# Context steps pinned behind the expert tile they are written beside, with other weights for the steps

## The chip, the cores and the metric

The kernel runs on one core of one Trainium2 chip. The metric is the time of one execution on the device in microseconds (us); the median of a few runs counts. PE or TensorE is the matrix engine, PEld its weight load, DVE, ACT and POOL are the vector, scalar and GpSimd engines, and SP is the queue that issues the loads of the weights.

## What is computed

Two blocks run one behind the other on 256 tokens of width 1024, in float32. The first mixes the tokens (mLSTM and Hyena) and ends in a mixture of 16 experts; each expert takes 32 tokens:

```python
aff = jax.nn.softmax((xn @ w_router).astype(jnp.float32), axis=-1)
g, idx = lax.top_k(jnp.swapaxes(aff, 1, 2), cap)
xs = xn[bidx, idx]
hid = jax.nn.silu(jnp.einsum('becd,edf->becf', xs, w_gate)) * jnp.einsum('becd,edf->becf', xs, w_up)
y = jnp.einsum('becf,efd->becd', hid, w_down) * g[..., None].astype(xn.dtype)
```

The second block has two layers and takes a context of 256 tokens beside the tokens `x`. Layer 0 carries the context through the whole layer, layer 1 only needs its keys and values:

```python
mod_c = silu_cc @ w_ada[l] + b_ada[l]
o, oc = token_mixers(modulate(x, sh1, sc1), modulate(xc, sh1c, sc1c), ...)
if ctx_out:
    xc = layer_norm(DEEPNORM_ALPHA * xc + g1c * (oc @ w_out[l]), ln1_g[l], ln1_b[l])
    xc = layer_norm(DEEPNORM_ALPHA * xc + g2c * swiglu(modulate(xc, sh2c, sc2c), ...), ln2_g[l], ln2_b[l])
```

`token_mixers` holds two softmax attentions of three pairs of heads each and a gated linear attention between them. The context depends on nothing that the first block computes.

## The kernel before, in words

The program has three stages. `phase_a` is the mixing of the first block, up to the router's scores. Then the experts and the context run together, driven by `run` (L446 to L486). Then `x_path` (L1906) is the second block for the tokens.

The expert stage. `moe` (L1112) is a generator: for each expert, 8 tiles of `w_gate`, 8 of `w_up` and 8 of `w_down`, 384 tiles in all, each 128 x 2048 floats (1 MB). A tile is loaded by `etile` into one of seven buffers (`w`, four, and `wb`, three) and used by four products of 32 x 512 (`xsel` or `hidT` against the tile), which appear in the profile as eight; after each tile `moe` yields. Between two experts `combine` (L1166) adds the result to the tokens (`Yh` and `Yl` against `PT`).

The context. `ctx_path` (L1874) is a generator too. First it runs what `self.later` still holds: the modulation vectors of both blocks (`modvec`, L399), for which tiles of `w_ada` (0.5 MB) go through four buffers `wm`. Then come the context's projections, the linear attention (`gla`, L1680, eight levels, each with keys scaled on DVE, POOL and ACT before TensorE makes the scores), the pairs of softmax attention (`pair_attn`, L1391: scores, softmax on DVE and ACT, `turn` for the transposes, `av` for the values), the output projection, a layer norm (`lnT`, L1183: `colsum`, `rows`, `colsum`, `rows`), the feed-forward part and another layer norm. Each part yields a number before it writes its instructions: what it is worth in expert tiles, where 1.43 make one tile.

`run` interleaves both in the text: after each expert tile it takes steps of the context until their sum has reached the share that belongs to the tile. That is only the order of writing. A scheduler behind it then orders the instructions of each engine by what it expects to be ready, so a step of the context may move ahead of expert tiles beside or before which it was written. Each engine executes its own list in order; SP issues the loads in its order, and one load that waits for a free buffer holds up those behind it. `issue_after(x)` makes the instructions that a block writes on the engine of `x` stand behind `x` in that list; other engines are not touched.

The names in the profile: `w` and `wb` are expert tiles, `wm` tiles of the context and of the modulation, `lhs` the modulation's input, `xsel` the chosen tokens, `hid` and `hidT` an expert's hidden values, `E` the scaled keys of the linear attention, `Pm` the softmax, `nak`, `naq`, `nav` and `gak`, `graw`, `gav` keys, queries and values of both attentions, `inv` the constant of the norm's sums, `nm` and `lnr` its means and roots.

Of the kernel before, what the change touches and what calls it, by code (L numbers as in the profile page):

```python
# [218 lines left out]
class _B:  # L219
# [104 lines left out]
    def T(self, pool, shape, tag, bufs=1, dt=F32):  # L324
        self.n += 1
        return pool.tile(shape, dt, tag=tag, name=f"{tag}_{self.n}", bufs=bufs)

    def P(self, tag):
        self.n += 1
        return self.pp.tile([128, 512], F32, tag=tag, name=f"ps{self.n}", bufs=self.pbufs[tag])  # L330
# [115 lines left out]
    def run(self):  # L446
        nc, tc, d = self.nc, self.tc, self.d
        self.wbufs = {"w": 4, "wm": 4, "wx": 2, "wb": 3, "wd": 2, "split": 4}
        with ExitStack() as es:
            E = lambda **k: es.enter_context(tc.tile_pool(**k))  # L450
            self.cp = E(name="cp", bufs=1)
            self.res = E(name="res", bufs=1)
            pm, pa = "b", "a"
            self.ws = E(name="ws", bufs=5, side="right")
            with tc.tile_pool(name="ps", bufs=1, space=PSUM) as self.pp, \
                    tc.tile_pool(name="wm", bufs=4, side="right") as self.wm:
                self.pbufs = {"b": 2, "a": 3, "g": 2, "f": 1}
                self.setup()
                with tc.tile_pool(name="A", bufs=1) as ap:
                    self.wx = ap  # L460
                    self.phase_a(ap, pm, pa)
                    self.wx = None
                if self.stop == "A":
                    return
                kp = E(name="kv", bufs=1)
                self.kvpool(kp)
                with tc.tile_pool(name="M", bufs=1) as mp, tc.tile_pool(name="WB", bufs=1) as self.wb:
                    self.moe_route(mp, pm)
                    with tc.tile_pool(name="X", bufs=1, side="right") as xp:

                        g = self.ctx_path(xp, pa)
                        done, total = 0.0, 480.0
                        for i, _ in enumerate(self.moe(mp, pm)):
                            while done < total * (i + 1) / 336:
                                c = next(g, None)
                                if c is None:
                                    break
                                done += c
                        for c in g:
                            done += c  # L480
            if self.stop == "X":
                return
            self.pbufs = {"g": 2, "l": 2, "s": 2, "t": 1, "o": 1}
            with tc.tile_pool(name="ps2", bufs=1, space=PSUM, reuse_waits="tile") as self.pp, \
                    tc.tile_pool(name="C", bufs=1, reuse_waits="tile") as xp:
                self.x_path(xp)  # L486
# [625 lines left out]
    def moe(self, mp, pm):  # L1112
        nc, T, P, d = self.nc, self.T, self.P, self.d
        m = self.mod1
        for e in range(16):
            xs = self.xsel[:, :, 32 * e:32 * e + 32]
            pp = []
            for w in ("w_gate", "w_up"):
                ps = P("g")
                for k in range(8):  # L1120
                    wt = self.etile(d[w][e, 128 * k:128 * k + 128, :])
                    for c in range(4):
                        self.mm(ps[32 * c:32 * c + 32, :], xs[:, k], wt[:, 512 * c:512 * c + 512], k == 0, k == 7)
                    yield
                pp.append(ps)

# [22 lines left out]
            for i in range(8):  # L1149
                wt = self.etile(d["w_down"][e, 256 * i:256 * i + 256, :].rearrange("(a p) c -> p a c", p=128))  # L1150
                for a in range(2):
                    kt = 2 * i + a
                    for n in range(2):
                        g = 2 * a + n
                        o = 128 * (kt % 4) + 32 * (kt // 4)
                        self.mm(py[32 * g:32 * g + 32, :], hT[:, o:o + 32], wt[:, a, 512 * n:512 * n + 512], i == 0, i == 7)
                yield
            Y = (keep[:, 512:1024], keep[:, 1024:1536]) if e == 15 else tuple(
                T(mp, [128, 512], "Y" + c, 1, F32R) for c in "hl")
# [22 lines left out]

    def lnT(self, p, psp, z, tag, outbufs=1):  # L1183

        yield 1.4
        ps = self.P(psp)
        self.colsum(ps, z, self.inv[:, 0:1])
        nm = self.T(p, [128, 2], "nm", 2)
        self.ts(nm, ps[:, 0:2], 0.5)
        pb = self.P(psp)  # L1190
        yield 1.4
        self.rows(pb, nm)
        sq = self.T(p, [128, 8, 256], tag)
        bc = pb[:, 0:256].unsqueeze(1).to_broadcast([128, 2, 256])
# [1 line left out]
            self.tt(z[:, k:k + 2], z[:, k:k + 2], bc, ALU.add)  # L1196
            self.act(sq[:, k:k + 2], z[:, k:k + 2], AF.Square)
        ps = self.P(psp)
        yield 2.8
        self.colsum(ps, sq, self.inv[:, 1:2])  # L1200
        r = self.rsqrt(p, ps[:, 0:2], 2, 1.0, 1e-5, "ln")
        pb = self.P(psp)
        yield 1.4
        self.rows(pb, r)
        bc = pb[:, 0:256].unsqueeze(1).to_broadcast([128, 2, 256])
        for k in range(0, 8, 2):
# [184 lines left out]
    def pair_attn(self, st, qT, kT, vs, bias, oT, blk, nk):  # L1391
# [12 lines left out]
        s = st["s"]  # L1404
        for t in range(2):
            if s:
                yield 1.4
            SS = [self.P(st["S"]) for b in range(2)]
            for i, x in enumerate(kT):
                for b in range(2):  # L1410
# [16 lines left out]
                    turn(t, b, Pm)  # L1427
            if s:

                yield 1.4  # L1430
                for b in range(2):
                    turn(t, b, PP[b])

# [4 lines left out]
                    self.mm(po[hs[b], 0:256], vs(b, k), PT[b][:, k], k == 0, k == nk - 1)  # L1438
            self.evac(st, oT, blk, po[:, 0:256])
        if s:  # L1440
            yield 1.4
        return av

    def mixers(self, st, l, u, kvonly=False):
# [235 lines left out]
    def gla(self, st, l, QK, cb, v, gg, oT):  # L1680
# [20 lines left out]
        A = T(p, [128, 4, 2, 32], "rt", st["b2"])  # L1701
        for i, h in enumerate((128, 64, 32, 16, 8, 4, 2, 1)):
            n = 128 // h
            yield 1.4
            E = T(p, [128, 2, 256], "E", st["b2"])
            F, B = (cb[:, r].rearrange("p (n u h) -> p n u h", n=n, u=2) for r in range(2))
            q, k = (E[:, r].rearrange("p (n u h) -> p n u h", n=n, u=2) for r in range(2))
# [2 lines left out]
            g = nc.gpsimd  # L1710
# [6 lines left out]
            self.tt(Q, E[:, 0:1].to_broadcast([128, 4, 256]), QB, ALU.mult)  # L1717
            self.tt(E[:, 1], E[:, 1], QK[:, 1], ALU.mult)
            if s:
                yield 2.8  # L1720
            if h == 128:
                for a in range(2):
                    ps = P(psp)
# [285 lines left out]
```

## Time and profile before

| what | value |
|---|---|
| median of 3 runs | 2211.62 us (2205.5 to 2215.53) |
| the profiled execution | 2214.84 us, its span 2213.1 us |
| PE busy | 1973.6 us, 89% |
| DVE, ACT, POOL busy | 967.2, 632.4, 291.4 us |
| moved by DMA | 666.31 MB, mean 301 GB/s |
| loads of expert tiles | 384 of 1024 KB |
| chain that ended last | PE 38%, DMA 17%, DVE 6% |

Busy time of PE counts a product from its start to its modelled end, so a PE that is 89% busy may still wait. The page's second part cuts the span into 40 slices of 55 us; the line of bandwidth is the one to read here. The chain that ended last follows from the last instruction back to what released each step; a share for a DMA in it means that the chain stood waiting for that load.

### The profile page before, as it was taken

To read this page: it belongs to the slowest core of one execution; us is meant where nothing else is said; L and a number is where in the kernel's file an instruction comes from. 1 tells how busy PE (TensorE), PEld (TensorE's weight loads), DVE (VectorE), ACT (ScalarE), POOL (GpSimd) and SP (SyncE) were. 2 spreads that over 40 slices of the span, in tenths; PEclk is the share of its full clock that TensorE was granted. 3 is DMA by queue.
4 is the path that set the end of the run, shared out by engine and by line. 5 is a ranking of instruction groups with operands and counts; after the bars stand their busy time and mean duration, and the time that the engine had idled before them with its cause. 6 is when DMAs were issued, how large, how long until landed. Compare 5 with 4: busy or idle time off the path is not lost.

```text
span 2213.1 us, 33010 instructions
## 1 busy us (share of the span) xinstructions
PE 1973.6 (89%) x13588; PEld 1375.1 (62%) x13588; DVE 967.2 (44%) x1919; ACT 632.4 (29%) x1093; POOL 291.4 (13%) x334
## 2 busy tenths in 40 slices
PE   7999889977868988989888898789999998998998
PEld 3777645633215555545545553167789998778998
DVE  5566322134301210111001220168679878868974
ACT  5434221112300100000000110055545446554543
POOL 0012000000000000000000000043053216206311
PEclk9999889998969899999999898679999999999999
DMA  9887789997999999999999899953236673214652
GB/s 351 305 302 280 256 332 414 414 416 256 343 416 415 383 414 415 415 417 414 414 415 417 335 409 411 415 215 121 80 143 240 231 253 144 86 68 174 229 198 86
DMA packets 133559, 666.31 MB, mean 301 GB/s; under 512 B 14624, under 2 KB 18144, under 8 KB 86944
## 3 DMA queue, kind: packets, MB, share of 16 engines
q1 hardware_dynamic: 132272, 660.38, 76.9%
q0 software_dynamic: 1136, 3.82, 0.5%
q8 instruction: 107, 1.75, 0.3%
q14 instruction: 44, 0.36, 0.0%
HBM read 663.10 MB, written 1.05 MB: 300 GB/s over the span
## 4 chain that ended last, share of the span: by engine, by line
PE 38%; DMA 17%; DVE 6%; POOL 2%; issue 2%; ACT 2%; SPq 0%; POOLq 0%; ACTq 0%; DVEq 0%
PE ps L236 36%; DMA wb<-in_w_up 4%; DMA wm<-in_w_f 4%; DMA w<-in_w_up 3%; DMA w<-in_w_down 3%; DMA wb<-in_w_down 3%; PE ps L306 1%; DVE wl L319 1%; POOL xT L319 1%; DVE ll L322 1%; DMA wd<-in_w_ada 1%; DMA wm<-in_w_in 1%; POOL xT L316 0%; DVE xT L322 0%; DVE xT L319 0%
## 5 line engine op out<-in xcount | busy, mean ns | idle before, releaser
L236 PE MATMUL ps<-u,wm 128*128 128x256 f32 (+1 forms) x1168 | 269.4, 389 | 4.4 <-DMA wm<-in_w_out 2.4
L236 PEld LDWEIGHTS ps<-u,wm 128*128 128x128 f32 (+1 forms) x1168 | 221.3, 192 | 70.8 <-issue 16.9
L319 DVE TENSOR_TENSOR wl<-w,wh 128x1024 fp32r<-128x1024 f32 (+1 forms) x194 | 239.6, 1244 | 55.3 <-ACT wh L309 55.0
L236 PE MATMUL ps<-lh,wh 128*128 128x258 f32 x848 | 244.9, 290 | 7.6 <-DVE lt L319 7.6
L236 PE MATMUL ps<-ll,wh 128*128 128x258 f32 x848 | 244.8, 289 | 5.2 <-DVE ll L322 5.2
L236 PE MATMUL ps<-lh,wl 128*128 128x258 f32 x848 | 244.2, 288 | 5.6 <-DVE wl L319 4.1
L309 ACT ACTIVATE wh<-w 128x1024 fp32r<-128x1024 f32 (+1 forms) x196 | 200.1, 1029 | 163.0 <-PE ps L236 153.3
L236 PE MATMUL ps<-w,xsel 128*32 128x512 f32 x1176 | 176.7, 642 | 28.3 <-DMA w<-in_w_up 18.6
L319 DVE TENSOR_TENSOR hid<-hid,ps 128x256 f32<-128x256 f32 (+1 forms) x38 | 20.2, 533 | 371.2 <-ACT hid L309 251.7
L236 PEld LDWEIGHTS ps<-lh,wh 128*128 128x128 f32 x848 | 164.5, 194 | 9.9 <-ACT wh L309 8.0
L236 PEld LDWEIGHTS ps<-ll,wh 128*128 128x128 f32 x848 | 165.0, 195 | 6.3 <-DVE ll L322 6.2
L236 PEld LDWEIGHTS ps<-lh,wl 128*128 128x128 f32 x848 | 164.5, 194 | 6.7 <-DVE wl L319 5.2
L236 PE MATMUL ps<-wb,xsel 128*32 128x512 f32 x872 | 130.3, 635 | 23.3 <-DMA wb<-in_w_up 21.4
L309 ACT ACTIVATE hid<-ps 128x256 f32<-128x256 f32 (+1 forms) x38 | 18.0, 474 | 403.1 <-PE ps L236 388.7
L236 PE MATMUL ps<-w,hidT 128*32 128x512 f32 x584 | 90.2, 718 | 30.1 <-DMA w<-in_w_down 23.1
L1129 POOL COPY px<-Pg 128x256 f32<-128x256 f32 x16 | 6.4, 400 | 743.4 <-PE ps L306 723.5
L236 PEld LDWEIGHTS ps<-w,xsel 128*32 128x32 f32 x1176 | 32.6, 111 | 113.4 <-issue 46.5
L236 PE MATMUL ps<-hidh,wl 128*128 128x256 f32 x352 | 98.6, 280 | 0.7 <-DVE wl L319 0.5
L236 PE MATMUL ps<-hidh,wh 128*128 128x256 f32 x352 | 98.8, 281 | 0.0
L236 PE MATMUL ps<-hidl,wh 128*128 128x256 f32 x352 | 98.3, 279 | 0.0
L322 DVE SCALAR_TENSOR_TENSOR xT<-ps,mod,xT 128x256 f32<-128x256 f32 x168 | 72.9, 478 | 57.4 <-PE ps L236 57.2
L319 POOL TENSOR_TENSOR hidl<-hj,hidh 128x256 fp32r<-128x256 f32 x44 | 66.0, 1501 | 152.3 <-ACT hidh L309 152.3
(476 smaller groups left out, 3662.8 us busy)
## 6 DMA issues: line engine op xcount, KB each, us to landing
w<-in_w_gate SPq DMA_DIRECT2D x74, 1024.0 KB, 15.6
w<-in_w_up SPq DMA_DIRECT2D x73, 1024.0 KB, 14.8
w<-in_w_down SPq DMA_DIRECT2D x73, 1024.0 KB, 15.9
w<-in_w_f SPq DMA_DIRECT2D x60, 1024.0 KB, 4.9
wb<-in_w_up SPq DMA_DIRECT2D x55, 1024.0 KB, 15.3
wb<-in_w_down SPq DMA_DIRECT2D x55, 1024.0 KB, 16.5
wb<-in_w_gate SPq DMA_DIRECT2D x54, 1024.0 KB, 15.5
wm<-in_w_ada SPq DMA_DIRECT2D x76, 512.0 KB, 6.7
```

Source lines behind the costliest of these rows:

```text
L236: self.lm = self.nc.tensor.matmul(out, lhsT, rhs, start=start, stop=stop)
L306: self.nc.tensor.transpose(out, in_, self.ident[:k, :k])
L309: self.nc.scalar.activation(out, in_, func, **kw)
L319: return (eng or self.nc.vector).tensor_tensor(out, a, b, op)
L322: return (eng or self.nc.vector).scalar_tensor_tensor(out, in0, s, in1, op0, op1)
L1129: nc.gpsimd.tensor_copy(px.rearrange("p t (r s) -> p t r s", r=4), self.Pg[:, :, e, :].unsqueeze(2).to_broadcast([128, 2, 4, 32]))
```

## The change

There are two edits. `moe` remembers its last product after each tile as `self.elm`, and `run` takes each step of the context under `issue_after(self.elm.ins)`: its instructions on TensorE stand behind the tile beside which it is written. And the numbers that steps yield are others: larger for the softmax steps and the layer norms, smaller for the linear attention, with the total and the number of tiles raised accordingly (1.43 still make a tile).

```diff
                         g = self.ctx_path(xp, pa)
-                        done, total = 0.0, 480.0
+                        done, total = 0.0, 524.4
                         for i, _ in enumerate(self.moe(mp, pm)):
-                            while done < total * (i + 1) / 336:
-                                c = next(g, None)
+                            while done < total * (i + 1) / 366:
+
+                                with tc.issue_after(self.elm.ins):
+                                    c = next(g, None)
                                 if c is None:
                                     break
                                 done += c
...
                         self.mm(ps[32 * c:32 * c + 32, :], xs[:, k], wt[:, 512 * c:512 * c + 512], k == 0, k == 7)
+                    self.elm = self.lm
                     yield
...
                         self.mm(py[32 * g:32 * g + 32, :], hT[:, o:o + 32], wt[:, a, 512 * n:512 * n + 512], i == 0, i == 7)
+                self.elm = self.lm
                 yield
...
     def lnT(self, p, psp, z, tag, outbufs=1):
-        yield 1.4
+        yield 2.8
...
         for t in range(2):
             if s:
-                yield 1.4
+                yield 2.6
...
         for i, h in enumerate((128, 64, 32, 16, 8, 4, 2, 1)):
             n = 128 // h
-            yield 1.4
+            yield 0.8
```

The other steps of `lnT` go from 1.4 to 2.8 and from 2.8 to 4.2, the other two of `pair_attn` from 1.4 to 2.6, and the second of a `gla` level from 2.8 to 1.6.

The first place is TensorE's list in the first softmax attention, before. `Pm` against the constants is a transpose, `nak` and `naq` make scores, `PT` and `nav` values, `w` and `wb` against `xsel` an expert tile.

```order
L236 MATMUL ps_4048<-w_4064,xsel_2704 32x512 x4
L306 MATMUL ps_4276<-pc_70,Pm_4258 128x128 x2
L306 MATMUL ps_4280<-pc_70,Pm_4265 128x128 x2
L236 MATMUL ps_4311<-nak_461_2686,naq_3621 128x256
L236 MATMUL ps_4312<-nak_461_2686,naq_3621 128x256
L236 MATMUL ps_4048<-wb_4070,xsel_2704 32x512 x4
L306 MATMUL ps_4335<-pc_70,Pm_4317 128x128 x2
L306 MATMUL ps_4339<-pc_70,Pm_4324 128x128 x2
```

The same place after:

```order
L236 MATMUL ps_4191<-nak_461_2686,naq_3615 128x256
L236 MATMUL ps_4192<-nak_461_2686,naq_3615 128x256
L236 MATMUL ps_4134<-w_4209,xsel_2704 32x512 x4
L236 MATMUL ps_4134<-w_4215,xsel_2704 32x512 x4
L306 MATMUL ps_4221<-pc_70,Pm_4197 128x128 x2
L306 MATMUL ps_4225<-pc_70,Pm_4204 128x128 x2
L236 MATMUL ps_4134<-w_4229,xsel_2704 32x512 x4
L236 MATMUL ps_4235<-w_4236,xsel_2704 32x512 x4
L236 MATMUL ps_4242<-nak_461_2686,naq_3615 128x256
L236 MATMUL ps_4243<-nak_461_2686,naq_3615 128x256
```

Where one expert tile stood between the scores and their transposes and none before the next scores, two and two stand now.

The second place is TensorE's list at the routing, before the first expert tile, in the kernel before. `aff` and `sl` are the router's probabilities and slots on their way through transposes, `oh` the one-hot matrix that chooses the tokens; `wm` against `lhs` is a modulation tile.

```order
L306 MATMUL ps_2902<-pc_70,mrow_2900 128x128 x2
L236 MATMUL ps_2907<-wm_2908,lhs_37_143 32x256
L306 MATMUL ps_2736<-pc_70,aff_2730 16x128 x2
L236 MATMUL ps_2907<-wm_2908,lhs_37_143 32x256 x3
L236 MATMUL ps_2907<-wm_2914,lhs_37_143 32x256 x4
L236 MATMUL ps_2907<-wm_2920,lhs_37_143 32x256 x4
L236 MATMUL ps_2907<-wm_2932,lhs_37_143 32x256 x4
L306 MATMUL ps_2756<-pc_70,sl_2752 128x16 x2
L236 MATMUL ps_2907<-wm_2938,lhs_37_143 32x256 x4
L236 MATMUL ps_2766<-oh_2761,xth_2718 128x512
```

After, the routing stands alone, and behind the first expert tile (`w_2819`) the modulation begins:

```order
L306 MATMUL ps_2736<-pc_70,aff_2730 16x128 x2
L306 MATMUL ps_2756<-pc_70,sl_2752 128x16 x2
L236 MATMUL ps_2766<-oh_2761,xth_2718 128x512
...
L236 MATMUL ps_2818<-w_2819,xsel_2704 32x512 x4
...
L236 MATMUL ps_2625<-wm_2852,lhs_37_143 32x256 x4
L236 MATMUL ps_2625<-wm_2858,lhs_37_143 32x256 x4
L236 MATMUL ps_2625<-wm_2864,lhs_37_143 32x256 x4
L236 MATMUL ps_2818<-w_2870,xsel_2704 32x512 x4
L236 MATMUL ps_2625<-wm_2876,lhs_37_143 32x256 x4
```

Eleven modulation tiles (`wm_2852` to `wm_2938`) moved from ahead of the first expert tile to behind it; between expert tile 8 and 9 stand fourteen of them now, where seven stood.

The third place is TensorE's list at the second layer norm, before. `inv` against `xcT` and `u` makes the sums, `nm` and `lnr` are spread over rows.

```order
L236 MATMUL ps_7387<-inv_76,xcT_2825 128x1 x10
L236 MATMUL ps_7406<-pc_70,nm_7404 128x128 x2
L236 MATMUL ps_7337<-w_7407,hidT_7335 32x512 x4
L236 MATMUL ps_7424<-inv_76,u_7415 128x1 x6
L236 MATMUL ps_7337<-w_7425,hidT_7335 32x512 x4
L236 MATMUL ps_7424<-inv_76,u_7415 128x1 x10
L236 MATMUL ps_7457<-pc_70,lnr_7455 128x128 x2
L236 MATMUL ps_7337<-w_7431,hidT_7335 32x512 x4
```

After:

```order
L236 MATMUL ps_7535<-inv_76,xcT_2825 128x1 x16
...
L236 MATMUL ps_7575<-wb_7576,hidT_7573 32x512 x4
L236 MATMUL ps_7575<-w_7582,hidT_7573 32x512 x4
L236 MATMUL ps_7554<-pc_70,nm_7552 128x128 x2
L236 MATMUL ps_7575<-w_7600,hidT_7573 32x512 x4
L236 MATMUL ps_7575<-w_7606,hidT_7573 32x512 x4
L236 MATMUL ps_7575<-w_7612,hidT_7573 32x512 x4
L236 MATMUL ps_7599<-inv_76,u_7590 128x1 x16
L236 MATMUL ps_7575<-wb_7639,hidT_7573 32x512 x4
L236 MATMUL ps_7575<-wb_7645,hidT_7573 32x512 x4
L236 MATMUL ps_7638<-pc_70,lnr_7636 128x128 x2
L236 MATMUL ps_7694<-u_7657,wm_7690 128x256 x4
```

The four steps stood with none or one expert tile between two of them; now two or three stand there, and the first product of layer 1 (`u` against `wm`) stands directly behind the last step. On SP the loads moved with their users: after expert tile 8's load, eighteen loads of modulation tiles stand in a row there.

## Rows read from the trace of the kernel before

**Rows 1.** The page's bandwidth in 40 equal slices of the span, GB/s.

```profile
GB/s 351 305 302 280 256 332 414 414 416 256 343 416 415 383 414 415 415 417 414 414 415 417 335 409 411 415 215 121 80 143 240 231 253 144 86 68 174 229 198 86
```

**Rows 2.** Stretches: busy us and count per engine (columns in its first line), clock, DMA.

```profile
core 0: us, PE busy (x) PEld busy (x) DVE busy (x) ACT busy (x) POOL busy (x), PEclk, DMA share, GB/s
350.00:500.00 150.00, 133.06 (x826) 78.69 (x828) 31.40 (x61) 20.26 (x38) 7.93 (x13) 0.97 1.02 415
500.00:600.00 100.00, 80.99 (x518) 32.09 (x510) 41.18 (x120) 31.16 (x86) 3.66 (x6) 0.90 0.79 287
600.00:730.00 130.00, 103.87 (x574) 46.19 (x568) 15.33 (x34) 5.50 (x9) 0.81 (x2) 0.82 1.02 416
730.00:770.00 40.00, 37.25 (x221) 21.83 (x221) 11.47 (x27) 5.98 (x12) 1.09 (x2) 0.90 0.95 370
1230.00:1310.00 80.00, 73.51 (x413) 41.95 (x410) 22.78 (x49) 17.32 (x27) 3.64 (x5) 0.86 0.93 357
312.00:1448.00 1136.00, 971.01 (x5592) 513.62 (x5596) 192.57 (x447) 113.62 (x231) 21.56 (x38) 0.91 0.99 398
```

**Rows 3.** Timeline of PE: start, us, instruction, count, [idle before <-releaser]; expert tiles alone.

```profile
624.69 1.94 PE L236 MATMUL ps<-w,xsel 128*32 128x512 f32 x8 [0.58 <-DMA w<-in_w_up]
627.18 1.76 PE L236 MATMUL ps<-w,xsel 128*32 128x512 f32 x8 [0.56 <-DMA w<-in_w_up]
```

**Rows 4.** Timeline of PE in the first softmax attention of the context.

```profile
539.93 1.54 PE L236 MATMUL ps<-PT,nav 128*64 128x256 f32 x8
541.40 0.70 PE L236 MATMUL ps<-nak,naq 64*128 64x256 f32 x4
542.03 1.06 PE L236 MATMUL ps<-wb,xsel 128*32 128x512 f32 x8
543.89 0.87 PE L306 MATMUL ps<-pc,Pm 128*128 128x128 f32 x4 [0.79 <-DVE sm L1423]
```

**Rows 5.** Timeline of PE: tile 57, a linear-attention level, first scores, tile 89.

```profile
462.67 1.06 PE L236 MATMUL ps<-w,xsel 128*32 128x512 f32 x8 [0.59 <-DMA w<-in_w_up]
...
499.50 1.08 PE L236 MATMUL ps<-PT,E 128*32 128x128 f32 x16 [2.73 <-DVE E L319]
...
522.77 1.21 PE L236 MATMUL ps<-nak,naq 64*128 64x256 f32 x2
...
587.13 1.06 PE L236 MATMUL ps<-wb,hidT 128*32 128x512 f32 x8
```

**Rows 6.** Timelines of DVE, ACT and PE, in this order, at the routing.

```profile
269.10 0.18 DVE L319 TENSOR_TENSOR aff<-lg,mx 128x32 f32<-128x32 f32 x1
...
272.75 0.19 DVE L319 TENSOR_TENSOR aff<-aff,sm 128x32 f32<-128x32 f32 x1
...
270.37 0.38 ACT L309 ACTIVATE mrow<-ps 128x256 f32<-128x256 f32 x1 [2.21 <-PE ps L236]
270.77 1.28 ACT L309 ACT_TABLE_LOAD   x1
272.07 0.23 ACT L309 ACTIVATE aff<-aff 128x32 f32<-128x32 f32 x1
...
269.23 1.08 PE L236 MATMUL ps<-wm,lhs 128*32 128x256 f32 x8 [3.42 <-DMA wm<-in_w_ada]
...
274.76 1.03 PE L236 MATMUL ps<-wm,lhs 128*32 128x256 f32 x2 [3.25 <-DMA wm<-in_w_ada]
275.72 0.60 PE L306 MATMUL ps<-pc,aff 128*16 128x128 f32 x2
```

**Rows 7.** Timeline of SP: issues of loads, the time that a row's issues took.

```profile
264.33 14.22 SPq L396 DMA_DIRECT2D wm<-in_w_ada  x6
...
299.06 9.45 SPq L396 DMA_DIRECT2D wm<-in_w_ada  x7
...
311.76 1.37 SPq L396 DMA_DIRECT2D w<-in_w_up  x3
```

**Rows 8.** Timeline of PE: modulation tiles between expert tile 8 and 9.

```profile
306.19 0.64 PE L236 MATMUL ps<-wm,lhs 128*32 128x256 f32 x8 [0.19 <-DMA wm<-in_w_ada]
...
314.10 1.08 PE L236 MATMUL ps<-wm,lhs 128*32 128x256 f32 x8 [0.20 <-DMA wm<-in_w_ada]
```

More of the change, by code (lines that the diff above doesn't have):

```diff
@@ L1190, in lnT @@
         pb = self.P(psp)
-        yield 1.4
+        yield 2.8
         self.rows(pb, nm)
@@ L1198, in lnT @@
         ps = self.P(psp)
-        yield 2.8
+        yield 4.2
         self.colsum(ps, sq, self.inv[:, 1:2])
@@ L1202, in lnT @@
         pb = self.P(psp)
-        yield 1.4
+        yield 2.8
         self.rows(pb, r)
@@ L1406, in pair_attn @@
             if s:
-                yield 1.4
+                yield 2.6
             SS = [self.P(st["S"]) for b in range(2)]
@@ L1428, in pair_attn @@
             if s:
-                yield 1.4
+                yield 2.6
                 for b in range(2):
@@ L1440, in pair_attn @@
         if s:
-            yield 1.4
+            yield 2.6
         return av
@@ L1703, in gla @@
             n = 128 // h
-            yield 1.4
+            yield 0.8
             E = T(p, [128, 2, 256], "E", st["b2"])
@@ L1719, in gla @@
             if s:
-                yield 2.8
+                yield 1.6
             if h == 128:
```

## The prediction

> **What bounds the kernel now.** I read the bandwidth line of the page first: from about a seventh to two thirds of the span most slices move 414 to 417 GB/s, and a few of them far less [rows 1]. So I took busy time by stretches [rows 2]. From 350 to 500 us and from 600 to 730 us the loads run at 415 and 416 GB/s; that is the expert stage with its 384 weight tiles of 1 MB, and TensorE's rows there wait for the next tile, which comes every 2.49 us (627.18 minus 624.69) while its products take 1.94 us at the lower clock [rows 3]. In this stage the loads set the pace, and the context's work stands beside them for nothing as long as TensorE comes back for the next tile before all weight buffers are full. Over the whole stage, 312 to 1448 us, the mean is only 398 GB/s. At 416 the same bytes take 1136 x 398 / 416 = 1087 us, so 49 us are lost, and the dips say where: 287 GB/s over 500 to 600 us loses 100 x (1 - 287/416) = 31.0 us, 370 over 730 to 770 loses 4.4, 357 over 1230 to 1310 loses 11.3. That is 46.7 of the 49.
>
> What stands there is the context's chains. In the attention stage a tile's products follow each other at one in 3.47 us (13 tiles from 542.03 to 587.13 [rows 4, 5]) where the loads would bring one in 2.49: each softmax step (scores, DVE and ACT in between, transposes) has one expert tile to hide behind, and the transposes still wait 0.79 us [rows 4]. The other two dips are the layer norms of the context, where the order puts three or four dependent steps between four expert tiles.
>
> From 1448 us on the kernel is another program (the second block), bound by TensorE; the order of its instructions does not change on any engine, so all of the difference has to come from the expert stage and its start.
>
> **The change, part by part.** Nothing is computed or loaded that was not before; only the order moves. The sum is made against the profiled execution, 2214.84 us.
>
> *Attention.* In the order before, the twelve softmax steps stand among 18 expert tiles (71 to 89); after, they stand between tile 77 and tile 132, two tiles between scores and transposes in ten of twelve cases. Two tiles take 4.98 us of loads; the chain that they must cover is what one tile of 0.9 us, the 0.79 us of waiting and the instructions around them cover now, 542.03 to 543.89, under 2 us [rows 4]. So here TensorE keeps the loads' pace, and even gains on it. What is not gone is the lag that the linear-attention levels before it build up. Their steps are bound by DVE, ACT and POOL (TensorE waits 2.73 us for the scaled keys before a level [rows 5]); the chain keeps its length, the change only puts twenty tiles in place of fourteen beside it (57 to 77, where it was 57 to 71) and moves the combination of an expert ahead of the first scores. The last tile that waited for data is number 57, at 462.67; the first scores stood at 522.77 behind tile 71. I put them at some 531 us (5 us for the combination, 3 for six more tiles), behind tile 77, due at 462.67 + 20 x 2.49 = 512.5. That is a lag of 17.5 us near 530. How much lag the weight buffers swallow follows from the stage before: tile 89 ran at 587.13, due at 462.67 + 32 x 2.49 = 542.4, a lag of 44.8 us of which 31.0 cost loads; so 13.8 us cost nothing (seven buffers are 17.4 us). About 4 us of the 31.0 stay. Gain 27, bounds 20 (the lower clock in this stage) and 31.
>
> *First layer norm.* Its four steps now have two or three tiles each (tiles 153 to 160) instead of one: gain 4 of 4.4, bounds 2 and 4.4. *Second layer norm and the start of layer 1*: the steps that stood at tiles 309 to 313 now stand at 328 to 335, two or three tiles apart. One place stays bare: the first products of layer 1 stand directly behind the last step's rows, so TensorE waits there for DVE and ACT, a few us that the buffers cover. Gain 10 of 11.3, bounds 5 and 11.3.
>
> *The start costs.* The pin also holds what was useful early. Eleven tiles of the modulation weights (0.5 MB each) ran on TensorE while the routing chain went through DVE; now they stand behind expert tile 1. That helps the routing itself: the scores were ready at 269.28, yet ACT first had to evacuate a modulation row that came at 270.37, then load its table, and took the exponential at 272.07; the probabilities were ready at 272.94, but their transpose stood on TensorE behind a modulation product that waited 3.25 us for its weights, and ran at 275.72 [rows 6]. Without these the exponential comes near 269.5 and the transpose near 270.4, and the whole chain to expert tile 1 comes 5.3 us earlier. Against that, between expert tile 1 and 8 stand eight modulation tiles instead of four (some 2.3 us), and between tile 8 and 9 fourteen instead of seven, with four buffers and nothing else in SP's queue until they are through: the loads of expert tile 9 and later were issued at 311.76, right behind the last of them [rows 7]. One of these tiles took 1.58 us (306.19 to 314.10, five tiles [rows 8]). Seven more are 11.1 us, less 5.3 plus 2.3: the stream of expert loads starts 8 us later. Bounds: 2 (1.26 us a tile at 416 GB/s, and part of the products hidden) and 14 (2.37 us a tile, six in 14.22 us as SP issued them at 264.33 [rows 7], without a head start it would be more). I take the 1.58, from the rows with the same four buffers and next to nothing beside them.
>
> *Sum.* 27 + 4 + 10 - 8 = 33 us: 2214.84 - 33 = 2182 against the profiled execution. The median of the three runs of before is 2211.62, 3 us under it, so the forecast for a median is **2179 us**.
>
> The Trainium skill speaks against such a gain in one place: "DMA: Bandwidth & Descriptors", under "Where 436 GB/s comes from", says that for transfers from HBM the memory's share of one core, about 358 GB/s, is what binds. By it the slices at 357 and 370 GB/s would already be full and only the attention's would have room, 100 x (1 - 287/358) = 20 us less the 8 of the start, 2200 us. The trace does not agree: 415 and 416 GB/s held for 280 us in two stretches [rows 2].
>
> **The rivals.**
>
> *The clock stays low.* TensorE has gaps in the expert stage, and in the stretch from 600 to 730 us, where only few context steps stand, its mean granted clock is 0.82, with tiles at 1.94 us [rows 2, 3]. If the spread-out attention ran at 1.2 GHz throughout, its 55 tiles would take 107 us, the twelve scores and transposes 12 x 2 x (0.63 + 0.87) = 36 us (541.40 to 542.03, and the 0.87 [rows 4]) and the six value products 6 x 2 x 1.47 = 18 (539.93 to 541.40): 161 us against 55 x 2.49 = 137 of loads. That gives 24 of the 27 us back: 2203. Against it: at such a load TensorE is busy without gaps, and in the rows of before the clock was 2.4 GHz in stretches that are busier than 600 to 730 (0.97 in 350 to 500 us). The Trainium skill, "TensorE: Matmul & The Clock Gate" under "HAM oscillation", describes such a kernel, in which waits for data between groups of matmuls bring the lower clock back each time; the 0.82 agrees.
>
> *Slower: the modulation loads stall the start.* At 269.23 and 274.76 two successive modulation tiles were 5.53 us apart, each waiting over 3 us for its load, with other transfers beside it [rows 6]. If the fourteen tiles between expert tile 8 and 9 turned at that rate, they would take 14 x 5.53 = 77 us instead of 11 for seven, and the start would cost 77 - 11 - 3 = 63 us: 41 of gains less 63 gives 2211.6 + 22 = 2234. It decides from (41 + 11 + 3) / 14 = 3.9 us a tile. Against it: next to nothing is beside them then, and 1.58 is what that gave.
>
> *No change.* The pin could be empty, if the order that it asks for is what the program had, or the dips could move elsewhere: a lag over 14 us built up at another place costs what was saved. The first is excluded by the order; for the second, the feed-forward chunks, with 32 context products each, stand five tiles apart before and after. It would give 2205 to 2212.
>
> *A lower ceiling of the loads.* If full rate could not be had beside context work, the time would lie between, as worked out above: 2200. 415 GB/s from 350 to 500 us was had beside TensorE work of 133 us in 150 [rows 2].
>
> *More.* If the attention loses nothing and the start costs 2: 31 + 4.4 + 11.3 - 2 = 45 us, 2167.
>
> **How the numbers follow.** Forecast as described, 2170 to 2190: 0.70. The clock, 2190 to 2203: 0.13. More, under 2170: 0.06. A lower ceiling: 0.01. No change: 0.06. Slower: 0.04. The bounds of the terms together give 20 + 2 + 5 - 14 = 13 to 45 us of gain, that is 2199 to 2167; with some us for the runs' own spread (2205.5 to 2215.5 before) I give 2166 to 2197. Half a per cent, 11 us, is about what a measurement can tell from no change; faster by more means under 2200.6: 0.70 + 0.06 + 0.01 and 0.11 of the clock's 0.13, so 0.88; same 0.08, slower 0.04.
>
> **What would show it.** In the profile after: bandwidth at 414 to 417 GB/s through the attention, which then lasts to some 655 us (tile 132, 462.67 + 75 x 2.49, and the later start), with at most one short dip before its first scores; no dip at the layer norms; the first expert product 5 us earlier; the loads of expert tile 9 issued near 320; the second block starting near 1415 us and lasting as long as before. The forecast is wrong if the attention shows tiles of 1.94 us without waits for data, if the start has modulation tiles more than 2 us apart, or if the second block becomes longer.

## The result, and the profile after

The changed kernel takes 2186.72 us (median of 4 runs, 2180.38 to 2190.2) against 2212.43 us before (2205.5 to 2215.53): the ratio is 0.988, with a 95% interval of 0.986 to 0.990. The profiled execution of after took 2185.51 us, its span 2183.8; the span of before was 2213.1, so 29.3 us went away between the two traces. The forecast was 2179 us and 33 us. One of the four executions of `pin_only` below took 2749.48 us at a mean granted clock of 0.64, where its others read 0.95, and stays out of its median.

The page's line of bandwidth of the changed kernel, 40 equal slices of its span (before: [rows 1]):

```profile
GB/s 355 299 304 280 257 239 410 415 418 410 417 416 414 415 418 415 414 415 418 414 412 415 417 384 406 409 186 88 68 157 257 240 243 144 72 85 174 227 192 87
```

The 256 and 343 of the attention and the 383 of the first layer norm are gone: from the seventh slice to the 23rd the loads run at 410 to 418. One dip is left, 384 in the 24th slice (the second layer norm), and a new one stands at the start: 239 in the sixth slice, where before had 332.

The same by stages, as busy us and count of PE, PEld, DVE, ACT and POOL, TensorE's granted clock (1 is full speed), DMA share and GB/s. Before:

```profile
280.00:500.00 220.00, 189.11 (x1184) 106.76 (x1188) 50.33 (x111) 41.51 (x69) 10.33 (x18) 0.94 0.99 398
500.00:670.00 170.00, 130.78 (x765) 45.53 (x758) 49.68 (x139) 33.05 (x89) 4.47 (x8) 0.82 0.88 340
670.00:800.00 130.00, 118.13 (x701) 71.30 (x700) 19.83 (x44) 10.96 (x21) 1.09 (x2) 0.95 1.00 400
...
1200.00:1330.00 130.00, 117.60 (x665) 68.50 (x663) 28.65 (x62) 18.60 (x29) 3.98 (x6) 0.89 0.96 378
1448.00:2213.00 765.00, 722.25 (x5728) 663.07 (x5720) 607.24 (x1102) 392.32 (x640) 239.55 (x219) 0.98 0.45 159
```

After:

```profile
280.00:500.00 220.00, 194.38 (x1195) 105.83 (x1194) 39.83 (x90) 39.36 (x66) 8.37 (x13) 0.92 0.96 379
500.00:670.00 170.00, 119.81 (x890) 40.08 (x890) 55.06 (x151) 39.03 (x97) 6.13 (x12) 0.94 1.02 415
670.00:800.00 130.00, 116.28 (x688) 66.92 (x684) 24.65 (x54) 11.81 (x21) 1.50 (x3) 0.93 1.02 415
800.00:1200.00 400.00, 351.15 (x2007) 204.50 (x2000) 41.06 (x90) 18.04 (x37) 2.02 (x5) 0.96 1.02 415
1200.00:1330.00 130.00, 120.66 (x687) 65.96 (x685) 28.53 (x61) 18.71 (x29) 2.41 (x5) 0.93 1.01 401
...
1418.00:2184.00 766.00, 723.26 (x5728) 663.17 (x5720) 607.11 (x1102) 392.58 (x640) 237.77 (x219) 0.97 0.45 159
```

Read as lost time, (1 - GB/s / 416) x length, the attention went from 31.1 us to 0.4, the stretch with the first layer norm from 5.0 to 0.3, the one with the second from 11.9 to 4.7, and the start from 9.5 to 19.6. That is 30.7 + 4.7 + 7.2 - 10.1 = 32.5 us for 29.3 measured; the windows stand at fixed times, while the work in them has moved by up to 30 us, so some us of difference are in the method (the start below is better read from the loads themselves). The second block has the same length.

In the attention TensorE now waits for loads, as it should. PE of the changed kernel, in the second softmax attention (start, us, instruction, count, idle before and its releaser):

```profile
606.02 1.90 PE L236 MATMUL ps<-w,xsel 128*32 128x512 f32 x8 [1.43 <-DMA w<-in_w_up]
607.85 1.12 PE L306 MATMUL ps<-pc,Pm 128*128 128x128 f32 x4
608.89 1.35 PE L236 MATMUL ps<-w,xsel 128*32 128x512 f32 x8
610.18 0.70 PE L236 MATMUL ps<-gak,graw 64*128 64x256 f32 x4
611.00 1.06 PE L236 MATMUL ps<-wb,xsel 128*32 128x512 f32 x8
613.49 1.06 PE L236 MATMUL ps<-wb,xsel 128*32 128x512 f32 x8 [1.42 <-DMA wb<-in_w_up]
```

From 606.02 to 613.49 three tiles pass in 7.47 us, the 2.49 us of [rows 3], with a scores step and a transposes step between them; the transposes (`Pm`) have no idle time before them here, where [rows 4] had 0.79 us for DVE. Two of these tiles wait 1.4 us for their load.

### The profile page after: what moved, and what is told of

Same layout as the page of the kernel before. It is cut to its first block, busy times and chain, and to the rows that moved or that the text cites. A ratio compares the mean times of both kernels' runs of the same rounds, so it can differ in the third digit from the quotient of the medians.

```text
span 2183.8 us, 33015 instructions
## 1 busy us (share of the span) xinstructions
PE 1945.7 (89%) x13588; PEld 1362.4 (62%) x13588; DVE 966.9 (44%) x1919; ACT 636.0 (29%) x1096; POOL 289.8 (13%) x334
## 4 chain that ended last, share of the span: by engine, by line
PE 50%; DMA 23%; DVE 8%; POOL 2%; ACT 2%; issue 2%; SPq 0%; POOLq 0%; ACTq 0%; DVEq 0%
PE ps L236 48%; DMA wm<-in_w_f 5%; DMA w<-in_w_up 4%; DMA w<-in_w_down 3%; DMA wb<-in_w_down 3%; DMA wb<-in_w_up 3%; PE ps L306 2%; DMA wm<-in_w_out 2%; DVE wl L319 1%; POOL xT L319 1%; DMA wm<-in_w_ada 1%; DVE ll L322 1%; DMA wd<-in_w_ada 1%; DMA wm<-in_w_in 1%; DMA wb<-in_w_gate 1%
## 5 line engine op out<-in xcount | busy, mean ns | idle before, releaser
L236 PE MATMUL ps<-w,hidT 128*32 128x512 f32 x584 | 82.6, 655 | 31.0 <-DMA w<-in_w_down 23.4
## 6 DMA issues: line engine op xcount, KB each, us to landing
wb<-in_w_down SPq DMA_DIRECT2D x55, 1024.0 KB, 16.6
```

The lines of the kernel that those rows point to most:

```text
L236: self.lm = self.nc.tensor.matmul(out, lhsT, rhs, start=start, stop=stop)
```

## Experiments

All times are medians; a ratio is that to runs of the kernel before on the same chip (2212.67 us in the first four experiments, 2210.87 in the next four, 2210.16 in the last two; 2212.43 beside the changed kernel). Times of different groups can therefore be compared to 2 or 3 us only.

### The pin without the new weights, and the new weights without the pin

`pin_only` is the kernel before with the pin alone:

```diff
-                                c = next(g, None)
+                                with tc.issue_after(self.elm.ins):
+                                    c = next(g, None)
```

> The pin alone, with the weights, the total and the number of tiles of before. Theory 1 (the pin does it): without the pin the scheduler draws the softmax steps together, however they are weighted; with it the twelve softmax steps and six value steps stand one expert tile apart, over 30 tiles instead of 18. 30 tiles bring 30 x 2.49 = 75 us of loads, and TensorE needs 12 x (0.63 + 0.87 + 0.79) + 6 x 1.5 + 30 x 1.06 = 68 us, so nearly all of the attention's 27 us are won, nothing at the layer norms (one tile between steps), and the start costs its 11 us: 2212 - 27 + 11 = 2196 us, bounds 2190 and 2204, with the slices of the attention over 400 GB/s and both layer norms near 360 to 375. Theory 2 (it takes two tiles beside each step): one tile between scores and transposes leaves the wait of 0.79 us and the lower clock, half of the attention's loss stays: 2208 or more.

Measured: 2193.39 us (3 runs), ratio 0.991 (0.989 to 0.993). Its stretches:

```profile
500.00:670.00 170.00, 133.91 (x950) 52.27 (x942) 57.74 (x156) 39.87 (x100) 6.91 (x14) 0.95 1.02 416
670.00:800.00 130.00, 116.58 (x696) 71.68 (x692) 23.83 (x53) 11.43 (x22) 1.49 (x3) 0.97 1.01 405
...
1200.00:1330.00 130.00, 116.45 (x688) 67.79 (x681) 29.82 (x65) 21.63 (x34) 4.60 (x7) 0.95 0.96 379
```

The attention is whole again, 416 GB/s, with one expert tile beside most steps; the second layer norm is where it was, 379, and the first is little better, 405 where before read 400 and the changed kernel 415. Theory 1 holds.

`weights_only` is the changed kernel without the pin:

```diff
-                                with tc.issue_after(self.elm.ins):
-                                    c = next(g, None)
+                                c = next(g, None)
```

> The new weights, total and number of tiles, without the pin. Theory 1 (the pin does it): the weights only change the order of writing, and TensorE's list has the softmax steps between tile 69 and 88 as in the kernel before, the layer norm steps one tile apart; no term of the sum is won and the start costs nothing: 2212 us, within 4, the attention at about 290 GB/s, the first expert product at 293 us. Theory 2 (the weights spread the steps and the pin only holds the start back): 2175 to 2185.

Measured: 2213.39 us (10 runs), ratio 1.000 (0.999 to 1.001). Its stretches:

```profile
500.00:670.00 170.00, 130.04 (x782) 42.81 (x774) 49.69 (x139) 33.01 (x89) 4.45 (x8) 0.83 0.89 345
...
1200.00:1330.00 130.00, 115.39 (x690) 66.03 (x691) 27.52 (x59) 16.61 (x25) 2.41 (x5) 0.96 1.02 408
```

The attention stays at 345 GB/s, 340 before: the weights write the softmax steps further apart, and the scheduler draws them together again (the first scores run at 523.04 us, 522.77 before [rows 5], and the last step of the attention at 587.51). One line is against theory 1: the second layer norm reads 408, not 378, without a pin. The profiled execution (2209.83 us) is some 5 us shorter than that of before, but the median of the ten is not; what that stretch is worth without the pin stays open.

### The start

`mod_free` takes the pin from the modulation steps alone:

```diff
-                                with tc.issue_after(self.elm.ins):
+                                pin = ExitStack() if self.free else tc.issue_after(self.elm.ins)
+                                with pin:
                                     c = next(g, None)
...
         yield from self.later
+        self.free = False
```

where `self.free` is true until then.

> The changed kernel with the pin taken from the modulation steps alone; from the context's own steps on everything is pinned. Theory 1 (the start's loss is the pinned modulation): 65 modulation tiles stand before the first expert tile again and 7 instead of 14 between tile 8 and 9, the routing is 5 to 6 us later, the loads of tile 9 are issued near 312 instead of 322.5, and the whole is 8 to 11 us shorter: 2177 us, bounds 2174 to 2181. Theory 2 (the later start is caught up, because the attention's lag needs that time or because the routing's lead is worth as much): 2187, within 3.

Measured: 2175.34 us, ratio 0.984 (0.982 to 0.985), 11.4 us less than the changed kernel, and better than both. What the pin does at the start is seen on SP's queue (issues of loads). The changed kernel:

```profile
262.85 1.72 SPq L396 DMA_DIRECT2D wb<-in_w_gate  x3
288.15 0.33 SPq L396 DMA_DIRECT2D w<-in_w_gate  x1
290.66 28.35 SPq L396 DMA_DIRECT2D wm<-in_w_ada  x18
...
322.54 1.38 SPq L396 DMA_DIRECT2D w<-in_w_up  x3
```

With unpinned modulation:

```profile
263.46 13.54 SPq L396 DMA_DIRECT2D wm<-in_w_ada  x6
...
277.58 4.57 SPq L396 DMA_DIRECT2D wm<-in_w_ada  x3
...
310.94 1.38 SPq L396 DMA_DIRECT2D w<-in_w_up  x3
```

In the changed kernel the queue stands from 264.57 to 288.15 at a load that needs the buffer of expert tile 1, whose products end at 288.09. Behind it stand the eleven modulation loads that `mod_free` issues ahead of that place (nine of them in its rows at 263.46 and 277.58): eighteen in a row, 1.58 us each. Meanwhile the routing runs with idle DMA engines; the stretch 276 to 288 us of the changed kernel, and then of `mod_free`:

```profile
276.00:288.00 12.00, 10.88 (x42) 7.85 (x42) 2.85 (x6) 6.23 (x8) 0.68 (x2) 0.76 0.01 2
```

```profile
276.00:288.00 12.00, 8.99 (x51) 5.75 (x44) 7.19 (x19) 2.71 (x4) 0.39 (x1) 0.75 0.90 334
```

2 GB/s against 334. `mod_route` pins the modulation steps behind the transposes of the router's probabilities, in order to have the early routing too (`self.ltp` is the last transpose):

```diff
+            self.relm = self.ltp
...
-                                with tc.issue_after(self.elm.ins):
+                                with tc.issue_after((self.relm if self.free else self.elm).ins):
```

> The changed kernel with the modulation steps pinned behind the transposes of the router's probabilities instead of behind expert tiles. The routing chain keeps its early start (exponential near 268.3, transposes near 269.3), 6 modulation tiles stand before the first expert tile, 5 up to tile 9, 11 behind it, where the changed kernel has none, 8 and 14. Theory 1: the loads of tile 9 are issued 4 to 7 us earlier than 322.5 and the whole is as much shorter: 2181 us, bounds 2178 to 2184, so less than with unpinned modulation, since 11 tiles stand in a row still. Theory 2 (the modulation's products in the routing hold it back by as much): 2187.

Measured: 2178.66 us, ratio 0.985 (0.984 to 0.986), between the two as expected. Its row of modulation loads has twelve, and the loads of tile 9 follow at 320.10:

```profile
298.43 17.08 SPq L396 DMA_DIRECT2D wm<-in_w_ada  x12
...
320.10 0.90 SPq L396 DMA_DIRECT2D w<-in_w_up  x2
```

That is only 2.4 us before the changed kernel's 322.54, not 4 to 7: one load of tile 9 to 16 (`w_up`, at 296.12) had gone ahead of the row, so that this place no longer measures the whole lead. The time fits theory 1; the place that I had named for it does not show it.

### The two weights

`attn_old` and `ln_old` are the changed kernel with one group of weights as before, in the softmax steps and in the layer norms:

```diff
             if s:
-                yield 2.6
+                yield 1.4
```

```diff
     def lnT(self, p, psp, z, tag, outbufs=1):
-        yield 2.8
+        yield 1.4
```

> The changed kernel with the softmax steps' weights of before, everything else of it kept: one expert tile beside most of these steps, where two stood. Theory 1 (the pin alone spreads them enough, as the pin with all weights of before suggested): the slices of the attention stay over 405 GB/s and the time is the changed kernel's, 2187 us, within 3. Theory 2 (the second tile is needed as soon as the linear attention before it is drawn together to two thirds): the lag of the linear attention is not worked off, the attention loses 5 us or more, 2192 to 2200.

Measured: 2188.43 us, ratio 0.989 (0.987 to 0.992), which cannot be told from the changed kernel; the attention reads 411 GB/s, with one slice of 402 where theory 1 had put all over 405.

```profile
500.00:670.00 170.00, 141.35 (x974) 62.99 (x974) 57.91 (x157) 37.52 (x95) 6.14 (x12) 0.95 1.01 411
```

> The changed kernel with the layer norms' weights of before, everything else of it kept: one or two expert tiles between their steps instead of two or three. Theory 1 (the layer norms' share of the gain comes from the weights): both dips come back, about 4 us at the first and 6 at the second, 2195 us, bounds 2192 and 2198. Theory 2 (the pin alone spreads them, as it does the softmax steps): 2187, within 3.

Measured: 2195.32 us, ratio 0.992 (0.989 to 0.995), 8.6 us more than the changed kernel. Its two layer norms:

```profile
670.00:800.00 130.00, 120.87 (x696) 69.93 (x697) 24.70 (x55) 12.67 (x22) 1.50 (x3) 0.92 1.02 415
1200.00:1330.00 130.00, 118.23 (x650) 67.49 (x650) 29.30 (x63) 18.60 (x29) 4.05 (x6) 0.89 0.94 370
```

So each theory is right for one norm: beside the pin and the other new weights the first is whole without weights of its own (415), the second needs them (370). The pin alone does not make the first whole (405 in `pin_only`). The smaller weights of the linear attention have no run of their own; `pin_only` and `ln_old`, which differ in them, in the softmax weights and in the total, are 2 us apart.

### The second layer norm, and the buffers

`ln_gap` is `mod_free` with one more step ahead of layer 1, so that its first products no longer stand directly behind the norm's last rows:

```diff
             else:
+                yield 4.2
                 self.affine(xp, self.xcT, col("ln2_g", 0, 8), ...)
```

> The changed kernel with unpinned modulation, and one more step, of weight 4.2, between the last step of the second layer norm and the first products of layer 1: three expert tiles and the combination of an expert stand there, where the products stood directly behind the rows. The changed kernel still lost (414 - 374) + (414 - 385) + (414 - 395) = 88 GB/s over 20 us each there, 88 / 414 x 20 = 4.3 us. Theory 1 (the bare place and the crowding behind it cost them): 3 to 4 us less than with unpinned modulation alone (2175), 2172 us, bounds 2170 and 2174, and the slices there over 400 GB/s. Theory 2 (they go to the low clock and the products of the norm's own sums, 3.7 us each, which stay): 2175, within 1.5.

Measured: 2174.99 us, ratio 0.983 (0.981 to 0.986), where `mod_free` had 0.984. The 3 to 4 us of theory 1 do not show, and two slices of 20 us still read 388 and 389 GB/s, so theory 1 is not borne out, though a cost of 1 or 2 us would be lost in runs that lie 5 us apart; the low clock and the sums that theory 2 names were not tried. To see whether it is a crowd of work on TensorE that loses the 4.6 us, `ln_wide` doubles the distance of this norm's steps instead (`s` multiplies the four weights), beside a second timing of `mod_free`:

```diff
-                yield from self.lnT(xp, "a", self.xcT, "u")
+                yield from self.lnT(xp, "a", self.xcT, "u", s=2)
```

> The changed kernel with unpinned modulation, and the weights of the second layer norm's four steps doubled: four to six expert tiles between two of them (tiles 330 to 344) instead of two or three (328 to 335). Unpinned modulation alone took 2175 us and lost (415 - 384) + (415 - 386) + (415 - 392) + (415 - 403) = 95 GB/s over 20 us each there, 4.6 us. Theory 1 (that loss is a crowd of TensorE work in a short stretch): it shrinks to 1 or 2 us, every 20 us there over 400 GB/s, 2172 us, bounds 2170 and 2174. Theory 2 (the steps' own waits and the work of layer 1 behind them lose it wherever they stand): 2175, within 1.5, the dip moved by some 20 us.

> The changed kernel with unpinned modulation once more, beside the one with wider layer norm steps, so that both stand against the same runs of before: 2175 us, bounds 2173 and 2178, whatever theory holds for the layer norm.

Measured: 2175.24 us, ratio 0.984 (0.981 to 0.986), beside 2174.95 us, ratio 0.984 (0.982 to 0.986). Again no difference. `ln_wide`, its lowest slice of 20 us and the whole stretch:

```profile
1280.00:1300.00 20.00, 15.93 (x94) 6.01 (x93) 5.78 (x14) 5.92 (x10) 0.72 (x1) 0.91 0.97 365
...
1200.00:1400.00 200.00, 175.36 (x1023) 93.13 (x1022) 36.95 (x81) 21.65 (x35) 4.62 (x7) 0.93 1.01 403
```

The same of `mod_free_2`:

```profile
1260.00:1280.00 20.00, 17.67 (x108) 9.34 (x106) 8.52 (x19) 7.42 (x14) 0.71 (x1) 0.89 0.98 366
...
1200.00:1400.00 200.00, 177.66 (x1030) 93.81 (x1026) 37.86 (x82) 22.34 (x36) 4.61 (x7) 0.92 1.01 403
```

The dip (366, then 365) moved 20 us along with the norm's last step (1270.14 us, then 1286.99), TensorE is not full in it (15.93 of 20 us), and the whole stretch reads 403 in both. That speaks against crowding; the loss moves with the last steps of the norm and the start of layer 1 behind them. What makes it stays open.

`five_buf` is the changed kernel with five weight buffers in place of seven:

```diff
-        self.wbufs = {"w": 4, "wm": 4, "wx": 2, "wb": 3, "wd": 2, "split": 4}
+        self.wbufs = {"w": 4, "wm": 4, "wx": 2, "wb": 1, "wd": 2, "split": 4}
```

> The changed kernel with five weight buffers in place of seven. Theory 1 (the lag that costs nothing is what the buffers hold): seven buffers swallowed 13.8 of the lag, five swallow 13.8 - 2 x 2.49 = 8.8 us; the lag of 10.6 us before the first scores then costs 2, other places that the seven hid (the second layer norm, the combinations of experts) some us more, and the start 3 to 5, since two tiles fewer are loaded ahead of the routing: 2196 us, bounds 2190 and 2206, with a deeper dip before the first scores (under 380 GB/s over 10 us). Theory 2 (the buffers are not what hides a lag, TensorE's reserve catches up by itself): no dip but the start's, 2188 to 2192.

Measured: 2205.78 us (10 runs), ratio 0.997 (0.996 to 0.998), 19.1 us more than with seven. Its stretches around the first scores:

```profile
490.00:510.00 20.00, 13.76 (x107) 4.61 (x105) 8.45 (x16) 7.43 (x13) 2.91 (x7) 0.91 0.92 371
510.00:520.00 10.00, 6.88 (x74) 2.56 (x72) 5.57 (x11) 1.75 (x4) 2.21 (x6) 0.83 0.92 353
...
530.00:540.00 10.00, 9.40 (x66) 5.08 (x66) 4.57 (x11) 2.26 (x5) 1.77 (x2) 1.00 0.85 333
```

From 520 to 530 us it reads 422. The same four stretches of the changed kernel read 409, 421, 409 and 394; its first scores run at 535.26, those of `five_buf` at 543.79, so the same work stands 8.5 us later here. With five buffers the stretches lose (45 x 20 + 63 x 10 + 83 x 10) / 416 = 5.7 us, with seven about 1: the lag (how far TensorE is behind the loads) of the linear attention and of the steps to the first scores is there in both, and the two buffers hide most of it. (The 10.6 us of the expectation left out two context loads; the lag is worked out anew below.) The dip before the first scores is 83 x 10 / 416 = 2.0 us, as expected; that the linear attention itself loses 3.7 us I had not named. More than half of the 19 us was lost elsewhere, part of it at the start (231 GB/s in 250 to 330 us where the changed kernel has 254: 80 x 23 / 416 = 4.4 us; and 406 from 330 to 490 us, where the changed kernel reads 415: 3.5 us); the rest I did not follow.

## Why the prediction was right, point by point

**What bounds the kernel: right.** The dips of [rows 2] were the time that could be won, and a stretch that reads 415 wins no more. The rule that about 358 GB/s from HBM is what binds (the Trainium skill, "DMA: Bandwidth & Descriptors", "Where 436 GB/s comes from") does not hold here, with one core running: the changed kernel moves 414 GB/s from 330 to 500 us and 415 from there to 1200.

**Attention: right that the spread steps let the loads keep their pace, wrong about what spreads them; forecast 27 us, measured 30.7.** It came from the pin, not from the two tiles: `pin_only` alone gives 416 GB/s and `weights_only` 345. The prediction put the gain on "two tiles between scores and transposes"; with one tile (`attn_old`, `pin_only`) the attention is all but as good (411 and 416 GB/s), since the pin alone spreads the steps over 30 tiles. In `attn_old` most transposes still wait 0.79 us for DVE behind their one tile, as before, so that wait was not the loss; the twelve steps in 18 tiles were. The 4 us that were to stay did not. The lag before the first scores was put at 17.5 us (its own terms, 522.77 + 5 + 3 - 512.5, give 18.3), and the trace has this:

```profile
474.89 1.04 PE L236 MATMUL ps<-w,xsel 128*32 128x512 f32 x8
...
535.26 0.70 PE L236 MATMUL ps<-nak,naq 64*128 64x256 f32 x4
535.90 1.92 PE L236 MATMUL ps<-w,xsel 128*32 128x512 f32 x16
...
538.55 1.92 PE L236 MATMUL ps<-w,xsel 128*32 128x512 f32 x16
...
543.25 1.06 PE L236 MATMUL ps<-wb,xsel 128*32 128x512 f32 x8 [1.15 <-DMA wb<-in_w_up]
```

The first row is tile 57, the last one tile 83, the sixth behind the first scores (x16 is two tiles, and tile 82 is not shown), and it waits for its load again. Six tiles took 543.25 - 535.26 = 8.0 us where loads bring them in 14.9, so the lag was 6.9 us. Two steps of the working failed. The first scores stand 60.4 us behind tile 57, as before (522.77 - 462.67 = 60.1 [rows 5]); the prediction had added 5 us for the combination and 3 for six tiles, but most of that went into time in which TensorE had stood idle: in these 60 us it is busy for 44.3 us, 38.8 before, and waits 12.6 us for the scaled keys, 15.6 before. And the due time of tile 77 left out two context loads of 0.5 MB that stand between the loads of tile 57 and 58. SP's queue of the kernel before, in its first row the load of expert tile 8, below it tile 57 and these two:

```profile
293.98 0.33 SPq L396 DMA_DIRECT2D w<-in_w_gate  x1
...
449.23 0.33 SPq L396 DMA_DIRECT2D w<-in_w_up  x1
449.61 0.90 SPq L396 DMA_DIRECT2D wm<-in_w_in  x2
```

Those two take 2.5 us, so the lag against loads at full rate is 60.4 - 20 x 2.49 - 2.5 = 8.1 us; the loads had themselves lost about 1 us by then (the 409, 421, 409 and 394 GB/s above), which leaves the 6.9. By the same 2.5 us the lag that the buffers swallowed was 11.3 rather than 13.8 us, an estimate from the one place in the kernel before. Five buffers would then swallow 6.3, and 8.1 would cost 1.8 us: the dip of `five_buf` is 2.0.

**First layer norm: forecast 4, measured 4.7.** The pin does it with this norm's weights of before, if the other weights are new (`ln_old`, 415 GB/s); with all weights of before it does about a third of it (`pin_only`, 405, between 400 and 415). So the two or three tiles that the prediction gave as the reason are not needed here, and which of the other weights helps was not tried. **Second layer norm: forecast 10, measured 7.2**; a mis-sized term. "No dip at the layer norms" was wrong: 374, 385 and 395 GB/s stand there, after. The bare place costs nothing that these runs can tell, as the prediction said (`ln_gap`); more distance gains nothing either (`ln_wide`). The changed kernel there:

```profile
1260.00:1280.00 20.00, 19.25 (x140) 10.66 (x132) 3.49 (x7) 3.02 (x5) 1.29 (x3) 0.79 0.99 374
1280.00:1300.00 20.00, 17.67 (x87) 7.82 (x84) 10.98 (x25) 6.01 (x10) 0.40 (x1) 0.95 1.00 385
1300.00:1320.00 20.00, 20.00 (x109) 11.19 (x108) 6.35 (x12) 7.38 (x10) 0.00 (x0) 1.00 1.02 395
```

**The start: forecast 8 lost, measured 11 to 12.** The routing came early as predicted. The first expert product before, and, after, the router's scores and the first expert product:

```profile
292.86 1.07 PE L236 MATMUL ps<-w,xsel 128*32 128x512 f32 x8
```

```profile
267.92 0.18 DVE L319 TENSOR_TENSOR aff<-lg,mx 128x32 f32<-128x32 f32 x1
...
287.03 1.06 PE L236 MATMUL ps<-w,xsel 128*32 128x512 f32 x8
```

That is 5.8 us, of which 1.2 stood there before the routing began (the scores came at 267.92, before at 269.10 [rows 6]); the chain itself became 4.7 us shorter, for 5.3. A modulation load in the row took 28.35 / 18 = 1.58 us, the value taken. The failed step is the count: the prediction charged seven more tiles at 1.58 us and 2.3 us for the rest, 13.4 in all, as TensorE's list has them. But loads are paced by SP's queue, and there all eleven moved into the row: from the issue of expert tile 8's load to those of tile 9 it was 17.8 us before (293.98, above, to 311.76 [rows 7]) and is 34.4 (288.15 to 322.54), 16.6 us more, which is eleven times 1.51. 16.6 - 4.7 = 11.9 us, and `mod_free` wins 11.4 by undoing it. That these loads had cost nothing beside the routing (334 GB/s against 2) is what the prediction should have priced. In both kernels two context loads stand between the last of these loads and those of tile 9, which its "nothing else in SP's queue" left out; they cancel. (Its lower bound of 2 us does not come out of its terms either: seven tiles at 1.26 us less 5.3 are 3.5.)

**Second block: right.** 765 and 766 us. It starts 30 us earlier than before, at 1418 us where 1415 was forecast.

**The sum.** With the sizes measured it is 31 + 5 + 7 - 12 = 31 us, for 29.3 between the spans; 3.7 us of the forecast's miss are there. That the sum came so near is in part luck: the attention gave 4 us more than forecast and the start took 4 more. The rest is how profiled executions stand to medians: that of before lay 3.2 us over the median shown then, and I took the same for after, whose profiled execution lies 1.2 us under its median (4.4 us together). So 2179 became 2186.72, inside the range.

**The rivals.** The clock did not stay low: it reads 0.94 from 500 to 670 us, and most tiles there take 1.06 us. The reason given against this rival was wrong all the same: TensorE was not "busy without gaps" but 70% busy (119.81 of 170 us), with waits of up to 1.5 us for loads. The modulation loads did not stall at 5.53 us a tile; they took 1.58. A lag that moves elsewhere (no change) is the one that came nearest: it is 6.9 us before the first scores, and with two buffers less it costs.

## What to carry to other kernels

Where a scheduler orders what a generator writes, numbers that space the steps may gain no time at all until something holds each step to its place; check in the order of instructions which of the two acts, and pin only the steps whose early start hurts. A step that is held back takes its loads along: count the loads that move in the queue that issues them, ask what hid them where they stood, and leave steps that have nothing but loads to wait for free to run ahead. And when a lag is estimated against due times, count every load in that queue, not only the tiles of the main stream.

## What the runs showed of the hardware

The loads kept 415 GB/s from 500 to 1200 us beside a TensorE that was 70% to 89% busy, so the context's work as such took no bandwidth away. The granted clock over 500 to 670 us rose from 0.82 before (0.83 in `weights_only`) to 0.94 in the changed kernel and 0.91 in `mod_free`. The mean before hides two levels:

```profile
550.00:600.00 50.00, 41.84 (x272) 15.06 (x264) 19.16 (x59) 19.66 (x54) 0.00 (x0) 1.00 0.87 319
600.00:650.00 50.00, 32.00 (x176) 5.45 (x170) 3.15 (x8) 1.20 (x2) 0.40 (x1) 0.72 1.02 417
```

In the crowded softmax steps, where TensorE waited for DVE, the clock read 1.00. After them it fell to 0.72, where expert tiles stood nearly alone and waited for their loads, as in [rows 3]. In the changed kernel tiles wait for loads too, by up to 1.5 us, but softmax steps stand between them, and the clock reads 0.91 from 600 to 620 us. From 500 to 520 us of the kernel before, in the linear attention with its waits of 2 to 3 us for DVE, it read 0.77. So a high and a low clock stand beside waits for DVE and beside waits for loads alike; what sets it was not tried.
